# A gate-weight quarter read and split earlier, and three tiles' sums moved from VectorE to GpSimd

## The chip, the cores and the metric

The kernel runs on one core of a Trainium2 chip. Its engines each run their own instruction list in order: TensorE (PE) for matrix products, VectorE (DVE) and ScalarE (ACT) for elementwise work, GpSimd (POOL) for a few elementwise operations and the indexed transfers, SyncE (SP) as the queue that issues most reads and writes of HBM. They meet through semaphores. The metric is the device time of one execution in microseconds (us), lower is better.

## What is computed

One decoder layer over 512 tokens of width 1024: three parallel mixers with a shared projection, a mixture-of-experts layer, then a gated per-layer embedding and a final norm. The change lies where the expert layer hands over to the last stage, so of the reference only this part matters:

```python
h = h + mix @ w_out[i]
# top-1 group of 8 experts, top-2 experts in it: 32 experts, 256 wide
hid = silu(t @ w_gate[e]) * (t @ w_up[e]) * combine
h = h + sum over e of hid @ w_down[e]
gate = sigmoid(rmsnorm(h, ple_norm_g) @ ple_gate_w + ple_gate_b)      # 1024 x 1024
e = p @ ple_proj_w                                                    # 256 -> 1024
h = h + gate * e
return rmsnorm(h, final_norm_g)
```

## The kernel before

The 512 tokens are four tiles of 128 (`h1[0]` to `h1[3]`, 128 x 1024 float32, resident in SBUF). The 32 experts run as 16 pairs. For each pair the tokens that chose it are gathered into 64 slots an expert; `gate_up` (L997) forms the two hidden products, `down` (L1029) the output product. The weights of a pair are six reads of 1 MB each, issued in order by SP from `load_units` (L691); each waits for the one three before it.

The outputs of pairs 0 to 14 are written by an indexed transfer to `yd` in HBM, two rows a token. They come back as `ys[t]` (1 MB a tile, `load_y`, L1168), and `add_y` (L1164) adds both rows to `h1[t]`: two 128 x 1024 additions, both inputs in SBUF. Pair 15 does not go through HBM: its result stays on the chip as a high part and a low part (L1038 on ScalarE, L1039 on VectorE), and `scatter` (L1051) brings it to the tokens with products against a one-hot matrix, the result in PSUM, which L1053 adds to half of `h1[t]`.

The gate product (L1242) runs with each float32 operand split into a high part `h` and a low part `l`: three products hi·hi, hi·lo, lo·hi for each of the 8 slices `k` of 128 rows, 24 matmuls of 512 columns for half a tile. The weights come as four quarters of 1 MB (`gate_load`, L1060). `gate_hi(k, hf)` (L1071, ScalarE) writes the high part of one slice and half, `gate_lo(k, hf)` (L1075, VectorE) the low part: 16 of each. The tokens are transposed by `turn` (L1221), whose high part is written by ScalarE (L1223) and whose low part by VectorE (L1224).

`finish` then takes each tile in two halves (the last one in three pieces): L1252 scales the product out of PSUM and adds the bias row, L1253 is the sigmoid, L1254 multiplies by the embedding, L1255 adds `h1`, L1256 sums squares, L1257 multiplies by the final gain. On VectorE L1254, L1255 and L1257 have both inputs in SBUF; L1252, L1053, L1039 and L1224 have one of theirs in PSUM. `rms` prepares a tile's norm; the powers -1/2 (`rsp`, `rsl`, L63) run on GpSimd.

The embedding product (`ple`, L724) is made of 32 quarter steps, each two products of 128 x 256, one PSUM bank for four of them; `PLE` says how many stand in each pair, `PLE_LAST` how many behind the last one.

The order on SP and PE is the order of the code; from pair 14 on so is that of ScalarE and VectorE. GpSimd's order is chosen by the scheduler. `unit` takes a 1 MB slot of a ring of SBUF buffers, `free` gives it back. The tail: `tail` calls `last(t)` for each tile, which runs the gate products, and at given steps `(half, k)` calls `prep(t + 1)` (the next tile's transposes, splits and norm) and `sums(t + 2)`.

Of the kernel before, what the change touches and what calls it, by code (L numbers as in the profile page):

```python
# [14 lines left out]
ALU = mybir.AluOpType  # L15
# [6 lines left out]
KC = D // P  # L22
# [5 lines left out]

FILL = (8, 3, 0, 1, 0, 1, 0, 1, 0, 1, 1, 1, 4, 2, 2, 2, 9)

PLE = (5, 1, 1, 1, 1, 1, 1, 1, 1, 1, 1, 1, 1, 1, 2)
PLE_LAST = (4, 4, 4)
AHEAD = 3
NR, NL = 4, 9
CLEAR = (7, 8, 9, 10)
# [578 lines left out]
def ffn(ctx, tc, A, K, mixh, mixl, out, dbg, stage):  # L614

    nc = tc.nc
    V, SC, PE, G = nc.vector, nc.scalar, nc.tensor, nc.gpsimd
# [7 lines left out]
    h1 = K["h1"]  # L625
# [10 lines left out]
    def unit(dt, shape, slot=None):  # L636
        slot = slot or ring.pop(0)
        u = slot[0].tile(shape, dt, name="unit", tag=slot[1])
        slot_of[id(u)] = slot, u
        return u  # L640

    def free(*us):
        ring.extend(slot_of[id(u)][0] for u in us)

    def big(n, dt=F32, shape=(P, D)):
        return mw.tile(list(shape), dt, name="big", tag=f"big{n}")
# [20 lines left out]
    ps = K["ps"]  # L667
# [17 lines left out]
    def load_units(m=96):  # L685

        while ring and m and len(slab) < 96:
            n, m = len(slab), m - 1
            n = n - n % 6 + (0, 3, 1, 4, 2, 5)[n % 6]
            slab[n] = unit(F32, [P, 2048])  # L690
            loads.append(nc.sync.dma_start(slab[n], A["w_exp"][n // 3, n % 3]).ins)  # L691
            if len(loads) > AHEAD:
                tc.add_manual_dep(loads[-1], loads[-1 - AHEAD].name,
                                  mybir.DependencyInfo(mybir.DependencyClass.Sync, mybir.DependencyReason.DATA))
# [20 lines left out]
    def ple_steps():  # L715

        pT, pW = pl_in
        for j in range(8):
            t, hf = j // 2, j % 2
            p = ps("pe", "sc" if j < 5 else "gu")  # L720
            for c in range(2):
                for k in range(2):
                    n = hf * 512 + c * 256
                    PE.matmul(p[:, c * 256:c * 256 + 256], pT[:, k * S + t * P:k * S + (t + 1) * P], pW[:, k, n:n + 256],  # L724
                              start=(k == 0), stop=(k == 1))
                    if c == k == 1:
                        kept.append((t, hf, p))
                        ple_out()
                    yield

    def ple_out():

        while kept and kept[0][0] // 2 < len(eo):
            t, hf, p = kept.pop(0)
            SC.activation(eo[t // 2][:, t % 2, hf * 512:hf * 512 + 512], p, AF.Copy)  # L735
# [3 lines left out]
    def ple(n):  # L739
        for _ in range(n):  # L740
            next(ple_left, None)
# [131 lines left out]
    with tc.manual_schedule(engines={mybir.EngineType.PE}):  # L873
        for hf in range(2):
            part(hf, 0, WO_LATE[:2])
        for n in range(len(halves) - 1):
# [5 lines left out]
            if n >= 2:  # L882
                t, hf = halves[n - 2]
# [130 lines left out]
    def down(i, behind=lambda n: None):  # L1014
        w, hid = hid_[i]
        pT = ps("ht", "ht")[:, :256].rearrange("p (f n) -> p f n", f=2)
        hT = mw.tile([P, 2, P], F32, name="hidT", tag="hidT")
        for f in range(2):
            PE.transpose(pT[:, f], hid[:, f * P:(f + 1) * P], ident)
        SC.activation(hT, pT, AF.Copy)  # L1020
        behind(0)
        o = out_[i] = []
        if i < 15:
            o = big(1)
        for hf in range(2):
            dn = ps("dn", "dn")
            for f in range(2):
                for e in range(2):
                    PE.matmul(dn[64 * e:64 * e + 64], hT[:, f, 64 * e:64 * e + 64],  # L1029
                              w[e][2][:, 1024 * f + 512 * hf:1024 * f + 512 * hf + 512],  # L1030
                              start=(f == 0), stop=(f == 1))
            if i < 15:
                SC.activation(o[:, 512 * hf:512 * hf + 512], dn, AF.Copy)  # L1033
                continue
            if hf == 0:
                o2 = unit(F32R, [P, 4, 512])
            oh, ol = o2[:, 2 * hf], o2[:, 2 * hf + 1]
            SC.activation(oh, dn, AF.Copy)  # L1038
            V.tensor_tensor(ol, dn, oh.bitcast(F32), ALU.subtract)  # L1039
            o.append((oh, ol))  # L1040
            behind(1 + hf)
        if i < 15:
            G.indirect_dma_start(out=yd, out_offset=bass.IndirectOffsetOnAxis(ap=idy[:, i:i + 1], axis=0), in_=o, in_offset=None,  # L1043
                                 bounds_check=2 * S - 1, oob_is_err=False)

    def scatter(j):

        t, hf = j // 2, j % 2
        sc = ps("sc", "sc")
        for q in range(2):  # L1050
            PE.matmul(sc, DTs[15][:, t], out_[15][hf][q], start=(q == 0), stop=(q == 1))  # L1051
        y = h1[t][:, 512 * hf:512 * hf + 512]
        V.tensor_tensor(y, y, sc, ALU.add)  # L1053


    gr, gw = [], {}
# [1 line left out]
    def gate_load(j):  # L1058
        gr.append(unit(F32, [P, 4, 512]))
        nc.sync.dma_start(gr[j], A["ple_gate_w"][j])  # L1060

    def gate_part(k, hf):
        hs = slice(hf * 512, hf * 512 + 512)
        return gr[2 * hf + k // 4][:, k % 4], gw[k][:, 0, hs], gw[k][:, 1, hs]

    def gate_hi(k, hf):

        if hf == 0:
            gw[k] = unit(F32R, [P, 2, D])
        raw, h, _ = gate_part(k, hf)  # L1070
        SC.activation(h, raw, AF.Copy, scale=g3c[:, k:k + 1])  # L1071

    def gate_lo(k, hf):
        raw, h, l = gate_part(k, hf)
        V.scalar_tensor_tensor(l, raw, g3c[:, k:k + 1], h.bitcast(F32), ALU.mult, ALU.subtract)  # L1075
        if k % 4 == 3:
            free(gr[2 * hf + k // 4])
# [54 lines left out]
    def count_beyond():  # L1132
        on = ov["on"] = mw.tile([1, 1], I32, name="on")
        po = ps("pov", "xt")
        PE.matmul(po[:1, :1], ov["om"], ones[:, :1], start=True, stop=True)
        V.tensor_copy(on, po[:1, :1])
# [22 lines left out]
    ys = []  # L1159

    def add_y(t, rs=(0, 1)):

        for r in rs:
            V.tensor_tensor(h1[t], h1[t], ys[t][:, r], ALU.add)  # L1164

    def load_y(t):
        ys.append(unit(F32, [P, 2, D]))
        nc.sync.dma_start(ys[t], yd.rearrange("(r n) d -> n r d", r=2)[t * P:(t + 1) * P])  # L1168

    ends = ExitStack()  # L1170
    for i in range(16):
        if i == 14:
            ends.enter_context(tc.manual_schedule(engines={mybir.EngineType.Activation, mybir.EngineType.DVE}))
        gate_up(i, between(i))
        free(slab[6 * i + 1], slab[6 * i + 4])
        if i == 15:
            break
        if i in (3, 7):
            eo.append(unit(F32, [P, 2, D]))
            ple_out()  # L1180
        load_units()
        if i == 0:
            ple(PLE[0])
        gather_T(i + 1, 1)
        if i > 0:
            ple(PLE[i])
        down(i, lambda n: gather_T(i + 1, 0))
        free(slab[6 * i + 2], slab[6 * i + 5])
        load_units()
        if i == 14:  # L1190
            load_y(0)
            for j in range(4):
                gate_load(j)
            load_y(1)
            rows = mix.tile([P, 2, D], F32, name="rows", tag="m0")
            nc.sync.dma_start(rows[:, 0], bcast(A["ple_gate_b"]))
            load_y(2)
            nc.sync.dma_start(rows[:, 1], bcast(A["final_norm_g"]))
            load_y(3)
# [33 lines left out]
    def prep(t):  # L1233
        for hf in range(2):
            turn(t, hf)()
        rms(t)
# [37 lines left out]
    def tail(sums=None):  # L1274

        for t in range(NT):
            at = {}
            if t + 1 < NT:
                at[1, 1] = lambda: prep(t + 1)
            if sums and t == 0:  # L1280
                at[0, 6] = lambda: sums(1)
            if sums and t + 2 < NT:
                at[1, 5] = lambda: sums(t + 2)
            last(t, at)

    def sums(t):
        add_y(t)
        for hf in range(2):
            scatter(2 * t + hf)

    down(15, lambda n: n < 2 and add_y(0, (n,)))
    ple(PLE_LAST[0])
    gate_hi(0, 0)
    for hf in range(2):
        scatter(hf)
    gate_lo(0, 0)
    gate_hi(1, 0)
    ple(PLE_LAST[1])
    lo = [turn(0, hf) for hf in range(2)]
    ple(PLE_LAST[2])  # L1300
    free(pl_in[1])
    for f in lo:
        f()
    gate_lo(1, 0)
    for k in range(2, KC):
        gate_hi(k, 0)
        gate_lo(k, 0)
    count_beyond()
    for k in range(KC):
        gate_hi(k, 1)  # L1310
        gate_lo(k, 1)
    ov_slots = ring[:3]
    junk, h3s = (unit(F32, shape, slot) for shape, slot in zip(([P, 2, 512], [P, 4, 512]), ring[3:]))
    SC.preload_act_table_set("sigmoid_and_others")
    rms(0)
    tail(sums)
    ends.close()
# [157 lines left out]
```

## Time and profile before

| what | value |
|---|---|
| median of 3 runs | 557.77 us (557.16 to 558.68) |
| the profiled execution | 556.99 us, of which span 555.2 us |
| TensorE busy, mean | 514.5 us (93%) |
| VectorE busy | 276.2 us (50%) |
| ScalarE busy | 210.8 us (38%) |
| GpSimd busy | 87.1 us (16%) |
| read from HBM | 139.61 MB |

All times of rows are us from the start of the span. The stages: mixers up to about 250 us, the expert pairs to 477 us, the rest is the stage that the change touches. A row of the timeline is one instruction or a run of equal ones: its start, how long it or the run lasted, its engine and line, what it writes and reads, how many (x14), and in brackets how long the engine had sat idle before it and what it waited for. A mean over the span tells little here: VectorE is busy for half the span, but nearly all the time in the last 75 us.

### The profile page before, as it was taken

What the parts mean: (1) busy time and instruction counts of PE and PEld (TensorE: products, weight loads), DVE (VectorE), ACT (ScalarE), POOL (GpSimd) and SP (SyncE); (2) the same over time, 40 slices, a digit from 0 to 9 for tenths busy, and PEclk for the clock granted to TensorE, in tenths of its full rate; (3) what the DMA queues carried; (4) which work ended last, traced back from release to release, by engine and by line L of the source; (5) the groups of instructions that cost most, each with busy time, mean ns of one, the idle gap of its engine ahead of it and who ended that gap; (6) DMA issues with size and microseconds to landing.
All of it is one profiled execution on the core that took longest, in us unless ns stands there. A gap on an engine that the chain in (4) does not pass through costs nothing.

```text
span 555.2 us, 7581 instructions
## 1 busy us (share of the span) xinstructions
PE 514.5 (93%) x2713; PEld 325.3 (59%) x2713; DVE 276.2 (50%) x735; ACT 210.8 (38%) x443; POOL 87.1 (16%) x122
## 2 busy tenths in 40 slices
PE   8899999999999999999999999998798987949992
PEld 5797886876997788844333333332233332638872
DVE  6762957756747565773422322221121111597764
ACT  7466665646766434411112111110111101473352
POOL 3301111221008500002111111111110000011110
PEclk9999999999999999999999999999999999988997
DMA  8882222300339669989999999999999999950111
GB/s 303 265 325 73 62 72 71 91 26 2 117 126 418 251 263 413 348 337 387 416 412 417 399 394 387 375 383 396 368 399 418 416 418 390 416 211 0 40 44 73
DMA packets 35641, 148.82 MB, mean 268 GB/s; under 512 B 6557, under 2 KB 14109, under 8 KB 22160
## 3 DMA queue, kind: packets, MB, share of 16 engines
q1 hardware_dynamic: 29984, 137.46, 64.3%
q0 software_dynamic: 4320, 7.95, 3.8%
q10 hardware_dynamic: 1296, 2.89, 1.3%
q8 instruction: 23, 0.38, 0.3%
q14 instruction: 18, 0.15, 0.1%
HBM read 139.61 MB, written 16.25 MB: 281 GB/s over the span
## 4 chain that ended last, share of the span: by engine, by line
PE 62%; DMA 18%; DVE 9%; ACT 7%; issue 2%; POOL 1%; SPq 0%; ACTq 0%; DVEq 0%; POOLq 0%
DMA unit<-in_w_exp_dram 17%; PE gu L997 12%; PE pj L234 9%; PE po L80 8%; PE dn L1029 7%; PE pj L257 5%; PE z L257 4%; PE z L311 2%; PE po L333 2%; PE pe L724 2%; ACT unit L1071 2%; PE x L974 1%; DVE h L1164 1%; PE pl L780 1%; PE z L292 1%
## 5 line engine op out<-in xcount | busy, mean ns | idle before, releaser
L997 PE MATMUL gu<-unit,xT 128*64 128x512 f32 x512 | 127.5, 598 | 13.1 <-DMA unit<-in_w_exp_dram 13.1
L997 PEld LDWEIGHTS gu<-unit,xT 128*64 128x64 f32 x512 | 37.0, 137 | 85.0 <-issue 59.2
L1029 PE MATMUL dn<-unit,hidT 128*64 128x512 f32 x256 | 60.6, 599 | 1.7 <-ACT hidT L1020 0.8
L234 PE MATMUL pj<-xh,wp 128*128 128x512 f32 x176 | 51.2, 398 | 0.4 <-ACT wp L69 0.4
L1242 PE MATMUL pg<-unit 128*128 128x512 f32 (+1 forms) x216 | 47.9, 378 | 0.8 <-ACT unit L735 0.6
L1002 ACT ACTIVATE sg<-gu 128x256 f32<-128x256 f32 x16 | 6.1, 383 | 110.5 <-PE gu L997 110.5
L1003 DVE SCALAR_TENSOR_TENSOR hid<-sg,wsl,gu 128x256 f32<-128x256 f32 x16 | 7.7, 478 | 79.6 <-ACT sg L1002 79.5
L1242 PEld LDWEIGHTS pg<-unit 128*128 128x128 f32 x216 | 37.9, 193 | 9.0 <-ACT unit L735 0.7
L1043 POOL DMA_INDIRECT yd<-big,idy x15 | 15.1, 1009 | 163.8 <-ACT big L1033 163.8
L1029 PEld LDWEIGHTS dn<-unit,hidT 128*64 128x64 f32 x256 | 19.7, 137 | 32.0 <-issue 24.2
L234 PEld LDWEIGHTS pj<-xh,wp 128*128 128x128 f32 x176 | 32.6, 188 | 8.2 <-ACT wp L69 1.3
L1033 ACT ACTIVATE big<-dn 128x512 f32<-128x512 f32 x30 | 17.9, 597 | 50.0 <-PE dn L1029 50.0
L930 DVE COPY SL<-sl 128x10 f32<-128x10 f32 (+1 forms) x17 | 2.8, 167 | 66.0 <-PE sl L929 66.0
L70 DVE TENSOR_TENSOR wp<-wraw,wp 128x768 fp32r<-128x768 f32 (+2 forms) x28 | 25.8, 927 | 13.6 <-ACT wp L69 13.4
L69 ACT ACTIVATE wp<-wraw 128x768 fp32r<-128x768 f32 (+2 forms) x28 | 22.8, 817 | 20.2 <-PE pj L234 9.8
L234 PE MATMUL pj<-xl,wp 128*128 128x512 f32 x88 | 29.4, 401 | 0.0
L986 DVE TENSOR_TENSOR xT<-xt,g2c 128x512 f32<-128x512 f32 x30 | 20.6, 687 | 11.8 <-PE xt L985 11.7
L80 PE MATMUL po<-wo,mx 128*128 128x512 f32 x96 | 25.7, 408 | 0.0
L257 PE MATMUL pj<-wp,xh 128*128 128x384 f32 x96 | 24.8, 351 | 0.0
L80 PE MATMUL po<-unit,mx 128*128 128x512 f32 x96 | 24.1, 399 | 0.0
L943 POOL DMA_INDIRECT xg<-tnd,idx x15 | 15.4, 1029 | 33.7 <-issue 16.0
L985 PEld LDWEIGHTS xt<-ident,xg 128*128 128x128 f32 x120 | 13.4, 141 | 11.5 <-issue 11.4
(293 smaller groups left out, 881.2 us busy)
## 6 DMA issues: line engine op xcount, KB each, us to landing
unit<-in_w_exp_dram SPq DMA_DIRECT2D x96, 1024.0 KB, 8.7
wraw<-in_w_in_dram SPq DMA_DIRECT2D x20, 384.0 KB, 3.5
yd<-zero SPq DMA_DIRECT2D x4, 1024.0 KB, 7.9
unit<-yd SPq DMA_DIRECT2D x4, 1024.0 KB, 6.5
unit<-in_ple_gate_w_dram SPq DMA_DIRECT2D x4, 1024.0 KB
wraw<-in_w_out_dram SPq DMA_DIRECT2D x8, 256.0 KB, 3.0
h<-in_x_dram SPq DMA_DIRECT2D x4, 512.0 KB
unit<-in_w_out_dram SPq DMA_DIRECT2D x4, 512.0 KB, 7.8
```

What stands on the lines that cost most here:

```text
L69: nc.scalar.activation(h, src, AF.Copy)
L70: nc.vector.tensor_tensor(l, src, h.bitcast(F32), ALU.subtract)
L80: nc.tensor.matmul(p, a[k][:, ts_], K["wo"][k][:, b, hs], start=(n == 0), stop=(n == 3 * len(ks) - 1))
L234: PE.matmul(q, a[:, i * P:(i + 1) * P], b[k], start=(n == 0), stop=(n == 3 * KC - 1))
L257: PE.matmul(p[t][:, :W_IN[j]], a[k][:, t * P:(t + 1) * P], b, start=(n == 0), stop=(n == 3 * KC - 1))
L943: G.indirect_dma_start(out=xg[i % 2], out_offset=None, in_=tnd, in_offset=bass.IndirectOffsetOnAxis(ap=idx[:, i:i + 1], axis=0), bounds_ch ...
L986: V.tensor_tensor(xTs[i, hf], p.rearrange("p (a b) -> p a b", a=4), g2c[:, 4 * hf:4 * hf + 4, None].to_broadcast([P, 4, P]), ALU.mult)
L997: PE.matmul(gu[64 * e:64 * e + 64], xTs[i, k // 4][:, k % 4, 64 * e:64 * e + 64], w[e][k // 4][:, 512 * (k % 4):512 * (k % 4) + 512], star ...
L1029: PE.matmul(dn[64 * e:64 * e + 64], hT[:, f, 64 * e:64 * e + 64], w[e][2][:, 1024 * f + 512 * hf:1024 * f + 512 * hf + 512], start=(f == 0 ...
L1033: SC.activation(o[:, 512 * hf:512 * hf + 512], dn, AF.Copy)
L1043: G.indirect_dma_start(out=yd, out_offset=bass.IndirectOffsetOnAxis(ap=idy[:, i:i + 1], axis=0), in_=o, in_offset=None, bounds_check=2 * S ...
L1242: PE.matmul(p, hT[t][:, a, ks], gw[k][:, b, hs], start=start and n == 0, stop=stop and n == len(ab) - 1)
```

## The change

The first quarter of the gate weights is read before the rows of tile 0 instead of behind them. ScalarE loads the sigmoid table and splits that quarter's four slices between the copy of pair 15's transposed hidden state and the copies of its output; VectorE does three of the four low parts there. Eight of the twelve quarter steps of the embedding product that stood behind the last pair move into pairs 6 to 13. The sums of tiles 1, 2 and 3 (`add_y`, six instructions) go from VectorE to GpSimd; in the code they are called earlier. `scatter` now issues only its product and returns the addition, so tile 1's product stands ahead of the gate products and its two additions behind the last low part. In tile 0 `prep(1)` moves from step (1, 1) to step (1, 6), `sums(2)` keeps (1, 5), and `sums(1)` at (0, 6) is gone.

```diff
-PLE = (5, 1, 1, 1, 1, 1, 1, 1, 1, 1, 1, 1, 1, 1, 2)
-PLE_LAST = (4, 4, 4)
+PLE = (5, 1, 1, 1, 1, 1, 2, 2, 2, 2, 2, 2, 2, 2, 2)
+PLE_LAST = 4
...
-            p = ps("pe", "sc" if j < 5 else "gu")
+            p = ps("pe", "sc" if j < 7 else "gu")
...
-        V.tensor_tensor(y, y, sc, ALU.add)
+        return lambda: V.tensor_tensor(y, y, sc, ALU.add)
...
-            V.tensor_tensor(h1[t], h1[t], ys[t][:, r], ALU.add)
+            (G if t else V).tensor_tensor(h1[t], h1[t], ys[t][:, r], ALU.add)
...
         if i == 14:
+            gate_load(0)
             load_y(0)
-            for j in range(4):
-                gate_load(j)
+            gate_load(1)
             load_y(1)
+            gate_load(2)
+            gate_load(3)
...
             if t + 1 < NT:
-                at[1, 1] = lambda: prep(t + 1)
-            if sums and t == 0:
-                at[0, 6] = lambda: sums(1)
+                at[1, 1 if t else 6] = lambda: prep(t + 1)
             if sums and t + 2 < NT:
+                at[0, 0] = lambda: add_y(t + 2)
                 at[1, 5] = lambda: sums(t + 2)
...
-    down(15, lambda n: n < 2 and add_y(0, (n,)))
-    ple(PLE_LAST[0])
-    gate_hi(0, 0)
...
+    def behind_down(n):
+        if n == 0:
+            SC.preload_act_table_set("sigmoid_and_others")
+            for k in range(4):
+                gate_hi(k, 0)
+            for k in range(3):
+                gate_lo(k, 0)
+        if n < 2:
+            add_y(0, (n,))
+
+    down(15, behind_down)
+    ple(PLE_LAST)
+    for f in [scatter(hf) for hf in range(2)]:
+        f()
+    gate_lo(3, 0)
     lo = [turn(0, hf) for hf in range(2)]
...
+    add_y(1)
     for f in lo:
         f()
-    gate_lo(1, 0)
-    for k in range(2, KC):
+    second = [scatter(2 + hf) for hf in range(2)]
+    for k in range(4, KC):
         gate_hi(k, 0)
         gate_lo(k, 0)
-    count_beyond()
     for k in range(KC):
         gate_hi(k, 1)
         gate_lo(k, 1)
+    for f in second:
+        f()
+    count_beyond()
...
-    SC.preload_act_table_set("sigmoid_and_others")
     rms(0)
     tail(sums)
```

In the rows of the order `unit` is a ring slot, `dn`, `pe`, `sc`, `xt` and `pg` are PSUM banks, `h_1_1509` is `h1[1]`, `ms` and `rsp` are columns of the norm. ScalarE behind the last pair, from the copy of its transposed hidden state (`hidT`) to the table load, the difference of the two orders:

```order
 L1020 ACTIVATE hidT<-ht 128x256
+L1293 ACT_TABLE_LOAD
+L1071 ACTIVATE unit<-unit,g3c 128x512 x4
 L1038 ACTIVATE unit<-dn 128x512 x2
 L735 ACTIVATE unit<-pe 128x512
-L1071 ACTIVATE unit<-unit,g3c 128x512 x2
-L735 ACTIVATE unit<-pe 128x512
-L1223 ACTIVATE unit<-xt 128x512 x2
-L735 ACTIVATE unit<-pe 128x512
-L1071 ACTIVATE unit<-unit,g3c 128x512 x14
-L1314 ACT_TABLE_LOAD
```

The table load and four of the sixteen high parts now stand ahead of the copies of the last output (L1038), and two of the copies of the embedding product (L735) are gone from here.

VectorE from the low parts of tile 0's transpose to the first step of `finish`, before:

```order
L1224 TENSOR_TENSOR unit<-xt,unit 128x512 x2
L1075 SCALAR_TENSOR_TENSOR unit<-unit,g3c 128x512 x7
L1136 CAST on<-pov 1x1
L1075 SCALAR_TENSOR_TENSOR unit<-unit,g3c 128x512 x8
L1208 TENSOR_SCALAR ms<-pm 128x1
L1210 SCALAR_TENSOR_TENSOR ms<-pm,ms 128x1
L1164 TENSOR_TENSOR h_1_1509<-h_1_1509,unit 128x1024 x2
L1053 TENSOR_TENSOR h_1_1509<-h_1_1509,sc 128x512 x2
L1252 SCALAR_TENSOR_TENSOR unit<-pg,rsp,rows 128x512
```

and now:

```order
L1226 TENSOR_TENSOR unit<-xt,unit 128x512 x2
L1075 SCALAR_TENSOR_TENSOR unit<-unit,g3c 128x512 x12
L1053 TENSOR_TENSOR h_1_1509<-h_1_1509,sc 128x512 x2
L1136 CAST on<-pov 1x1
L1210 TENSOR_SCALAR ms<-pm 128x1
L1212 SCALAR_TENSOR_TENSOR ms<-pm,ms 128x1
L1254 SCALAR_TENSOR_TENSOR unit<-pg,rsp,rows 128x512
```

Twelve low parts are left instead of fifteen, the two sums of tile 1 (L1164) are gone, and the two additions from PSUM stand ahead of the norm. (From here on the changed kernel's lines are two higher: L1252 is now L1254.)

GpSimd behind its last indexed transfer, the difference:

```order
 L943 DMA xg<-tnd,idx 128x1024
 L1043 DMA yd<-big,idy 1024x1024 x2
+L1164 TENSOR_TENSOR h_1_1509<-h_1_1509,unit 128x1024 x2
+L1164 TENSOR_TENSOR h_2_1510<-h_2_1510,unit 128x1024
+L63 TENSOR_TENSOR rsp<-ms,mhalf 128x1
+L1164 TENSOR_TENSOR h_2_1510<-h_2_1510,unit 128x1024
+L1164 TENSOR_TENSOR h_3_1511<-h_3_1511,unit 128x1024 x2
+L63 TENSOR_TENSOR rsp<-ms,mhalf 128x1
+L63 TENSOR_TENSOR rsl<-ms,mhalf 128x1
```

Three of the six sums stand ahead of tile 0's power (`rsp`), three behind it; nothing but the arrival of their rows and their own order holds them back.

## Rows read from the trace of the kernel before

**Rows 1.** Queue SP: timeline from 400 us (start, us, what), then its waits (total, times, longest).

```profile
401.44 62.83 SPq L691 DMA_DIRECT2D unit<-in_w_exp_dram  x24
...
SPq L691 <- DMA unit<-in_w_exp_dram: 39.9, 17, 3.2
```

**Rows 2.** Timeline, 472 to 485 us: start, us, instruction, count, idle time before it.

```profile
472.72 0.38 ACT L1020 ACTIVATE hidT<-ht 128x256 f32<-128x256 f32 x1 [1.05 <-PE ht L1019]
...
474.75 1.23 DVE L1164 TENSOR_TENSOR h<-h,unit 128x1024 f32<-128x1024 f32 x1 [2.57 <-DMA unit<-yd]
...
475.14 0.60 ACT L1038 ACTIVATE unit<-dn 128x512 fp32r<-128x512 f32 x1 [2.04 <-PE dn L1029]
...
479.25 1.29 DVE L1053 TENSOR_TENSOR h<-h,sc 128x512 f32<-128x512 f32 x2 [0.94 <-PE sc L1051]
...
482.10 1.89 PE L724 MATMUL pe<-unit,big 128*128 128x256 f32 x8
...
482.55 1.29 DVE L1224 TENSOR_TENSOR unit<-xt,unit 128x512 fp32r<-128x512 f32 x2 [1.35 <-ACT unit L1223]
```

**Rows 3.** Timeline, 484 to 500 us.

```profile
484.52 8.68 ACT L1071 ACTIVATE unit<-unit,g3c 128x512 fp32r<-128x512 f32 x14
...
489.32 5.37 DVE L1075 SCALAR_TENSOR_TENSOR unit<-unit,g3c 128x512 fp32r<-128x512 f32 x8
...
493.23 1.28 ACT L1314 ACT_TABLE_LOAD   x1
...
495.96 2.48 DVE L1164 TENSOR_TENSOR h<-h,unit 128x1024 f32<-128x1024 f32 x2
496.13 1.48 POOL L63 TENSOR_TENSOR rsp<-ms,mhalf 128x1 f32<-128x1 f32 x1 [34.43 <-DVE ms L1210]
498.54 1.29 DVE L1053 TENSOR_TENSOR h<-h,sc 128x512 f32<-128x512 f32 x2
```

**Rows 4.** Timeline of the tail: first step of each half tile, and others.

```profile
499.75 0.74 DVE L1252 SCALAR_TENSOR_TENSOR unit<-pg,rsp,rows 128x512 f32<-128x512 f32 x1
...
501.25 0.69 DVE L1254 TENSOR_TENSOR unit<-unit 128x512 f32<-128x512 f32 x1 [0.76 <-ACT unit L1253]
...
514.56 0.74 DVE L1252 SCALAR_TENSOR_TENSOR unit<-pg,rsp,rows 128x512 f32<-128x512 f32 x1
...
529.25 0.74 DVE L1252 SCALAR_TENSOR_TENSOR unit<-pg,rsp,rows 128x512 f32<-128x512 f32 x1
...
540.16 0.74 DVE L1252 SCALAR_TENSOR_TENSOR unit<-pg,rsp,rows 128x512 f32<-128x512 f32 x1
...
546.38 0.48 DVE L1252 SCALAR_TENSOR_TENSOR unit<-pg,rsp,rows 128x256 f32<-128x256 f32 x1
...
549.04 0.54 POOL L63 TENSOR_TENSOR rsl<-ms,mhalf 128x1 f32<-128x1 f32 x1 [9.38 <-DVE ms L1210]
```

**Rows 5.** Timeline of earlier stages: GpSimd and VectorE elementwise work side by side.

```profile
10.01 0.75 DVE L179 SCALAR_TENSOR_TENSOR xl<-xr,g,xh 128x512 fp32r<-128x512 f32 x1 [0.18 <-ACT xh L178]
...
16.13 2.04 POOL L183 TENSOR_TENSOR gs<-gs,xr 128x512 f32<-128x512 f32 x1 [2.07 <-ACT xr L181]
...
16.94 1.78 DVE L179 SCALAR_TENSOR_TENSOR xl<-xr,g,xh 128x512 fp32r<-128x512 f32 x1
...
175.14 2.38 POOL L677 TENSOR_TENSOR unit<-unit 128x1024 fp32r<-128x1024 f32 x1
175.26 0.69 DVE L85 TENSOR_TENSOR h<-h,po 128x512 f32<-128x512 f32 x1 [0.17 <-PE po L80]
```

**Rows 6.** Matmuls of the tail (timeline), then stretches: busy by engine, granted clock, DMA.

```profile
499.29 1.97 PE L1221 MATMUL xt<-ident,h 128*128 128x128 f32 x8 [7.18 <-DVE h L1053]
...
505.91 8.50 PE L1242 MATMUL pg<-unit 128*128 128x512 f32 x36
...
492.00:497.00 5.00, 0.11 (x1) 0.00 (x0) 3.96 (x8) 3.83 (x7) 0.87 (x1) 0.97 0.26 104
497.00:500.00 3.00, 0.71 (x4) 0.71 (x5) 2.86 (x5) 0.00 (x0) 0.61 (x1) 0.50 0.00 0
```

More of the change, by code (lines that the diff above doesn't have):

```diff
@@ L1286, in sums @@
     def sums(t):
-        add_y(t)
         for hf in range(2):
-            scatter(2 * t + hf)
-    down(15, lambda n: n < 2 and add_y(0, (n,)))
-    ple(PLE_LAST[0])
-    gate_hi(0, 0)
[L1294 to L1298, printed above, removed]
+            scatter(2 * t + hf)()
+    def behind_down(n):
[12 more added lines that the diff above has]
+    gate_lo(3, 0)
     lo = [turn(0, hf) for hf in range(2)]
-    ple(PLE_LAST[2])
     free(pl_in[1])
+    add_y(1)
     for f in lo:
         f()
-    gate_lo(1, 0)
-    for k in range(2, KC):
+    second = [scatter(2 + hf) for hf in range(2)]
+    for k in range(4, KC):
         gate_hi(k, 0)
         gate_lo(k, 0)
-    count_beyond()
     for k in range(KC):
```

## The prediction

> **What bounds the kernel now.** I read the read queue first. From 401.44 us it issues 24 reads of 1 MB in 62.83 us, 2.62 us each, and in the last part it waits for nothing but earlier reads [rows 1]. So up to pair 15 the stream of weights is the bound, and TensorE work there is free as long as it fits between reads. Then the timeline behind the last pair [rows 2]: ScalarE copies the hidden state until 473.10, tile 0's rows land at 474.75, the output is split, added to tile 0 by 479.25 + 1.29 = 480.54, and the transpose's low parts are done at 482.55 + 1.29 = 483.84. Then [rows 3]: ScalarE writes the last 14 high parts in 8.68 us (0.62 each), VectorE the last eight low parts in 5.37 us (0.67 each), ending at 489.32 + 5.37 = 494.69, behind ScalarE's 493.20. VectorE is the later of the two. Table load, norm, the sums of tile 1 (2.48) and its additions from PSUM (1.29) follow, and tile 0 is finished from 499.75 on. The tail is VectorE's step by step [rows 4]: the tiles start at 499.75, 514.56, 529.25 and 540.16, so 14.81, 14.69 and 10.91 us apart, and the last piece at 546.38, 6.22 later. The third distance is shorter by about what tile 3 no longer has: 2.48 + 1.29 = 3.77. So every microsecond off VectorE counts here until TensorE is the later one. TensorE needs 8.50/36 = 0.236 us a matmul [rows 6], 48 x 0.236 = 11.3 us a tile, plus about 1 us of transposes (eight took 1.97 at a halved clock) and about 1 us for the four products of a later tile: 13.4 us, only 1.3 below VectorE's 14.7.
>
> **The sum's frame.** It is made on the profiled execution: its time is 556.99, span 555.2, 1.8 around it. What follows the last piece (546.38 to 555.2) is not changed. The median of the runs, 557.77, is 0.78 above that execution, so I add the change of the last piece's start to 557.77.
>
> **Quarter steps of the embedding product.** Eight steps of 1.89/4 = 0.47 us [rows 2] leave the stage behind the last pair, one each for pairs 6 to 13. There the queue waits for reads only [rows 1], so they cost 0; without that cover, 8 x 0.47 = 3.8. What they give is in the ladder below, since ScalarE and VectorE set that stage.
>
> **The quarter read ahead.** It stands behind all weights in one queue, so I charge the weights nothing; if reads shared the bandwidth, up to one read's 2.62. It takes the place of tile 0's rows: it lands at or a little ahead of 474.75, since it doesn't wait for pair 14's output to be written. Tile 0's rows land one read later, 477.3 at most, tile 1's two reads after that, at about 482, tile 2's near 491.5 (two more quarters, half a read of bias rows and their own 1 MB), tile 3's near 495.
>
> **Behind the last pair.** ScalarE: 473.10, table load 1.28 [rows 3], four high parts 2.5, so the two output copies start at 476.9 instead of 475.14 and end at 478.1. VectorE: three low parts from 475.1 to 477.2, where it had mostly waited; two sums of 1.23 and two splits of 0.68, 481.0; two additions, 482.3 instead of 480.54. That is 1.8 late. The fourth low part and the transpose's two end at 484.2 instead of 483.84. Twelve low parts at 0.67 then end at 492.2, against 494.69: **2.5 saved**, if nothing holds VectorE.
>
> **The sums on GpSimd.** This is the term that decides. GpSimd takes 2.38 us for an operation of this shape with two inputs [rows 5], VectorE 2.48/2 = 1.24 [rows 3]; six of them are 14.3 us. The question is what VectorE does meanwhile. In an early stage, GpSimd ran an addition until 16.13 + 2.04 = 18.17; VectorE's split of the very form of the low part (both inputs in SBUF) had started at 16.94 and took 1.78 us instead of 0.75: it ended 0.55 behind GpSimd [rows 5]. An addition with one input in PSUM ran in 0.69 us right through a GpSimd operation of 2.38 [rows 5]. And GpSimd's tiny power took 1.48 us while VectorE added two SBUF rows [rows 3], 0.54 when it didn't [rows 4]. So the two exclude each other when VectorE reads two inputs from SBUF, and the one that waits gets its turn at the next end of an instruction. The Trainium skill says the same ("SBUF — State Buffer", Who interferes with whom): VectorE with two SBUF inputs contends with a GpSimd instruction that reads SBUF, and the second fully blocks until the first ends; by that rule the sums come out as forecast here, and the trace agrees (1.78 against 0.75). Its "Perfetto Trace Analysis" (Optimizing Scalar/DVE Operations) warns that moving work between these two engines might not help.
>
> Each sum therefore costs VectorE between 0 (beside a step on PSUM, or a wait) and about 2.2 us (2.38 less the start-up that overlaps), against 1.24 before. Placed by the arrivals: tile 1's first sum asks near 482, beside additions and low parts from PSUM: I take 0.8. Its second one, and tile 2's first near 491.5, fall into low parts: 2.2 each. Together 5.2, so the low parts end at 492.2 + 5.2 = 497.4. Two additions from PSUM 1.2, norm columns 0.4, power 0.54 and its hand-over: tile 0 starts at 499.6 instead of 499.75, **0.15 saved**. The 2.5 gained by the early quarter and the 2.48 of tile 1's sums go into the holding.
>
> **Tile 0.** Its 14.81 us lose 2.48 of sums and 0.6 of waits (the additions now stand where VectorE waited for ScalarE). The three sums left on GpSimd start with the tile. In L1254, L1255, L1257 VectorE reads two SBUF inputs, and each must wait for a sum: the first ends 0.55 behind 2.3, the second at 5.65, the third at 8.4 us instead of 3.65: 4.75 added. 14.81 - 2.48 - 0.6 + 4.75 = 16.5.
>
> **Tiles 1 to 3.** VectorE would need 14.69 - 2.48 = 12.2, but TensorE begins a tile only when its transposed low parts are there and needs 13.4, of which it is ahead by some tenths: 13.0. Tile 2 has no additions: 11.3 + 1 = 12.3 of TensorE instead of 10.91, since it is no longer ahead. The last step stays 6.2. **Sum:** 499.6 + 16.5 + 13.0 + 12.3 + 6.2 = 547.6 against 546.38, 1.2 later: 557.77 + 1.2 = **559.0**.
>
> **The rivals.**
> *No holding* (chance 0.15): GpSimd's long additions leave VectorE alone. For it: the short spans of GpSimd are rough in a profile. Against: the rows above. Low parts end at 492.2, tile 0 starts at 494.5, its step is 11.6 (VectorE without sums and waits), then 13.0, 12.3, 6.2: 537.6, 8.8 earlier, 549.0.
> *Half of it* (0.12): VectorE wins its turns, and sums fall beside steps on PSUM or waits for the sigmoid (0.76 in each half [rows 4]). If half of the 5.2 and 4.75 goes, 5.0 us: 554.0.
> *The clock of TensorE* (0.28), the slower side. Between tile 0's last product, near 501, and tile 1's low parts, near 509.5, TensorE has almost nothing. In the trace of before it had one matmul in 492 to 497; the granted clock was then 0.50 in 497 to 500 [rows 6], which is 1.2 GHz instead of 2.4, and eight transposes took 1.97. If tile 1's first 4 us of products run at that level they lose 2 us; 0.4 is slack, 1.6 counts, since tiles 1 and 2 are TensorE's: 560.6. It decides where such a gap arises again; the one before, 7.18 us of waiting, came ahead of the transposes [rows 6].
> *The quarter comes late* (0.05): if it lands a read later, at 477.3, the output copies and all behind shift by up to 2; part of it hides in the holding: 560.
>
> **How the numbers follow.** The forecast has 0.40. A measurement can tell about 0.3% from no change, 1.67 us, so the bounds are 556.1 and 559.4; the forecast lies just inside. Its uncertainty is about 1.5 us, mostly where tile 1's rows land: 1 us later or earlier moves the end by as much. Slower: 0.35 of the forecast, 0.8 of the clock, 0.6 of the late quarter, 0.39. Faster: the first rival, 0.8 of the second, a little of the forecast, 0.27. The rest, 0.34, is within. The range leaves out no holding below and the worst of the clock case above: 552.5 to 562.0.
>
> **What would show it.** Low parts (L1075) of 2.9 us instead of 0.74, two or three of them, and three steps of 1.4 us and more in tile 0's first half, each ending 0.55 behind a GpSimd sum; tile 0 starting near 499.6; tiles 16.5, 13.0 and 12.3 apart, TensorE without idle time in tiles 1 and 2. Right on the clock rival: a granted clock of 0.5 near 510. Wrong: low parts at 0.74 throughout and a start near 494.5.

## The result and the profile of the changed kernel

The changed kernel took 559.73 us (median of 6 runs, 558.47 to 562.25), the kernel before 556.94 in the same comparison: ratio 1.0055, 95% interval 1.0029 to 1.0081. It is slower by a little, by about 3 us. A second comparison (run e12 below) gave 1.0054 [1.0027, 1.0082].

The end of the weight stream moves by a microsecond or two from execution to execution, and all behind it moves along. So positions are counted here from the copy of pair 15's transposed hidden state, 472.72 in the kernel before [rows 2] and 471.65 in the changed one. From there to the last piece the kernel before takes 546.38 - 472.72 = 73.66, the changed one 547.91 - 471.65 = 76.26: 2.6 later. A position is read from one traced execution, a ratio from the medians of several.

The changed kernel's timeline behind the last pair; the columns are as in [rows 2], L1075 are the low parts, L1164 the sums:

```profile
471.65 0.38 ACT L1020 ACTIVATE hidT<-ht 128x256 f32<-128x256 f32 x1 [1.04 <-PE ht L1019]
...
474.24 2.56 ACT L1071 ACTIVATE unit<-unit,g3c 128x512 fp32r<-128x512 f32 x4 [0.91 <-DMA unit<-in_ple_gate_w_dram]
...
481.73 2.96 DVE L1075 SCALAR_TENSOR_TENSOR unit<-unit,g3c 128x512 fp32r<-128x512 f32 x1
...
485.82 11.10 DVE L1075 SCALAR_TENSOR_TENSOR unit<-unit,g3c 128x512 fp32r<-128x512 f32 x12
```

and GpSimd beside it:

```profile
481.78 5.16 POOL L1164 TENSOR_TENSOR h<-h,unit 128x1024 f32<-128x1024 f32 x2 [19.25 <-DMA unit<-yd]
490.53 2.52 POOL L1164 TENSOR_TENSOR h<-h,unit 128x1024 f32<-128x1024 f32 x1 [3.60 <-DMA unit<-yd]
```

The low part that starts beside GpSimd's first sum takes 2.96 us; in a run of them they stood 0.67 apart [rows 3], and a single one without a sum beside it takes 0.74. The next twelve take 11.10 where a version without sums (e2) takes 8.05. Together (2.96 - 0.74) + (11.10 - 8.05) = 5.3 us of holding. By sums it is 2.2 for the first, 0.9 for the second, which holds only the first of the twelve (it ends at 481.78 + 5.16 = 486.94), and 2.1 for the third, which starts at 490.53.

VectorE and GpSimd at tile 0, then the first step of the later tiles and of the last piece (L1254 is L1252 of the kernel before, and so on):

```profile
499.13 7.89 POOL L1164 TENSOR_TENSOR h<-h,unit 128x1024 f32<-128x1024 f32 x3
499.18 0.75 DVE L1254 SCALAR_TENSOR_TENSOR unit<-pg,rsp,rows 128x512 f32<-128x512 f32 x1 [0.68 <-POOL rsp L63]
...
500.69 1.37 DVE L1256 TENSOR_TENSOR unit<-unit 128x512 f32<-128x512 f32 x1 [0.76 <-ACT unit L1255]
502.10 2.71 DVE L1257 TENSOR_TENSOR unit<-unit,h 128x512 f32<-128x512 f32 x1
504.84 2.73 DVE L1259 TENSOR_TENSOR unit<-unit,rows 128x512 f32<-128x512 f32 x1
...
516.77 0.75 DVE L1254 SCALAR_TENSOR_TENSOR unit<-pg,rsp,rows 128x512 f32<-128x512 f32 x1 [1.41 <-PE pg L1244]
...
529.70 0.75 DVE L1254 SCALAR_TENSOR_TENSOR unit<-pg,rsp,rows 128x512 f32<-128x512 f32 x1 [0.47 <-PE pg L1244]
...
541.69 0.75 DVE L1254 SCALAR_TENSOR_TENSOR unit<-pg,rsp,rows 128x512 f32<-128x512 f32 x1 [0.45 <-PE pg L1244]
...
547.91 0.48 DVE L1254 SCALAR_TENSOR_TENSOR unit<-pg,rsp,rows 128x256 f32<-128x256 f32 x1
```

The three steps with two SBUF inputs take 1.37, 2.71 and 2.73 instead of 0.69 each [rows 4]: 4.74 more. The tiles are 17.59, 12.93 and 11.99 apart and the last piece 6.22 behind, against 14.81, 14.69, 10.91 and 6.22 [rows 4]. In [rows 4] no step waits for TensorE; here the first step of tiles 1, 2 and 3 does.

TensorE's timeline where tile 1 begins, and three stretches (columns: stretch, its length, busy of PE, PEld, DVE, ACT, POOL, granted clock, DMA share, GB/s):

```profile
500.23 1.64 PE L1244 MATMUL pg<-unit 128*128 128x512 f32 x6
...
506.16 0.73 PE L1244 MATMUL pg<-unit 128*128 128x512 f32 x2 [4.29 <-ACT unit L1225]
509.48 7.93 PE L1244 MATMUL pg<-unit 128*128 128x512 f32 x25 [2.60 <-DVE unit L1226]
```

```profile
504.00:508.00 4.00, 0.73 (x2) 0.30 (x2) 3.96 (x4) 2.91 (x8) 2.94 (x2) 0.85 0.00 0
508.00:512.00 4.00, 2.52 (x6) 2.04 (x7) 3.19 (x8) 0.63 (x1) 0.55 (x1) 0.50 0.00 0
512.00:516.00 4.00, 4.00 (x15) 3.17 (x15) 2.51 (x5) 1.34 (x3) 0.55 (x1) 0.80 0.00 0
```

TensorE stands still for most of 501.9 to 509.5. It first waits for tile 1's high parts, which ScalarE writes (L1225) only behind the squares of a step that VectorE ended late, then for tile 1's low parts, which VectorE itself reaches late (L1226). When it returns it runs at a granted clock of 0.50, the 1.2 GHz level, and the 25 products take 7.93 us, against 6.08 in a kernel where the clock stays at 1.00 (e2): 1.85 lost.

### The profile page after: what moved, and what is told of

It is laid out like the page before. It is cut to its first block, busy times and chain, and to the rows that moved or that the text cites. A ratio compares the mean times of both kernels' runs of the same rounds, so it can differ in the third digit from the quotient of the medians.

```text
span 556.7 us, 7586 instructions
## 1 busy us (share of the span) xinstructions
PE 515.1 (93%) x2713; PEld 325.4 (58%) x2713; DVE 280.0 (50%) x729; ACT 210.5 (38%) x443; POOL 99.9 (18%) x128
## 4 chain that ended last, share of the span: by engine, by line
PE 60%; DMA 25%; DVE 7%; issue 3%; ACT 3%; POOL 1%; SPq 0%; ACTq 0%; DVEq 0%; POOLq 0%
DMA unit<-in_w_exp_dram 18%; PE gu L997 10%; PE pj L234 9%; PE po L80 7%; PE dn L1029 6%; PE pg L1244 5%; PE pj L257 5%; PE z L257 4%; PE z L311 2%; DMA unit<-in_ple_gate_w_dram 2%; PE po L333 2%; DMA tnd<-big 2%; DVE unit L1075 1%; DMA yd<-big,idy 1%; DMA xr<-in_xT_dram 1%
## 5 line engine op out<-in xcount | busy, mean ns | idle before, releaser
L1244 PE MATMUL pg<-unit 128*128 128x512 f32 (+1 forms) x216 | 49.9, 390 | 6.9 <-ACT unit L1225 4.3
L1244 PEld LDWEIGHTS pg<-unit 128*128 128x128 f32 x216 | 39.5, 200 | 18.2 <-ACT unit L1225 4.7
L1029 PEld LDWEIGHTS dn<-unit,hidT 128*64 128x64 f32 x256 | 18.1, 136 | 33.7 <-issue 25.4
```

The costliest lines, as they stand in the source:

```text
L1244: PE.matmul(p, hT[t][:, a, ks], gw[k][:, b, hs], start=start and n == 0, stop=stop and n == len(ab) - 1)
```

## The experiments

Theory: GpSimd's sums hold every VectorE step that has two inputs in SBUF, and the late tile 1 then costs TensorE its clock. Rivals: the early quarter or the new order is at fault; the sums cost the same wherever they run; any GpSimd work slows VectorE; the clock is hidden. Each run was compared with the kernel before on the same chip. In the table, positions are from the copy of the hidden state (ACT L1020) of the same execution; "restart" is TensorE's first product that needs tile 1's low parts from VectorE.

| kernel | ratio, 95% interval | tile 0 starts | restart behind it | 25 products | last piece |
|---|---|---|---|---|---|
| before | 1 | 27.03 | | | 73.66 |
| changed | 1.0055 [1.0029, 1.0081] | 27.53 | 10.30 | 7.93 | 76.26 |
| changed again (e12) | 1.0054 [1.0027, 1.0082] | 27.54 | 10.31 | 7.83 | 76.18 |
| sums on VectorE (e1) | 0.9948 [0.9925, 0.9970] | 26.83 | 5.77 | 6.08 | 70.01 |
| the same again (e8) | 0.9915 [0.9887, 0.9943] | 25.78 | 5.77 | 7.01 | 69.05 |
| no sums (e2) | 0.9877 [0.9850, 0.9904] | 22.10 | 5.78 | 6.08 | 64.46 |
| quarter only (e3) | 0.9960 [0.9937, 0.9984] | 24.74 | | | 71.39 |
| sums only (e4) | 1.0078 [1.0051, 1.0105] | 31.89 | | | 76.64 |
| pause filled, 30 (e5) | 1.0025 [0.9999, 1.0050] | 27.48 | | | 75.48 |
| pause filled, 24 (e11) | 1.0009 [0.9987, 1.0032] | 27.51 | | | 74.47 |
| write only (e6) | 0.9850 [0.9799, 0.9901] | 22.48 | 5.78 | 7.62 | 66.39 |
| beside PSUM (e7) | 0.9938 [0.9917, 0.9958] | 26.05 | 5.77 | 7.38 | 69.69 |
| sums later (e9) | 0.9931 [0.9907, 0.9955] | 24.69 | 5.78 | 7.62 | 69.90 |
| later and filled (e10) | 0.9924 [0.9903, 0.9946] | 24.42 | | | 71.18 |

e1 and e8 are one kernel, and yet tile 0 starts 1.05 apart in them. Two arrivals make up most of it: ScalarE's first high part starts 2.59 behind the copy in e1 and 2.10 in e8, and in e1 VectorE waits another 0.47 for tile 0's rows. (That first high part starts 2.22 behind in e2, 2.57 to 2.61 behind in all others that read the quarter early.) So a difference of about 1 in the last column is read below only where the steps of the two traces show where it arises.

### Where the sums run (e1, e8, e2)

```diff
-            (G if t else V).tensor_tensor(h1[t], h1[t], ys[t][:, r], ALU.add)
+            V.tensor_tensor(h1[t], h1[t], ys[t][:, r], ALU.add)
```

> The changed kernel with the six sums of tiles 1 to 3 back on VectorE, at the places in the order where the change calls them; all else as changed. Holding theory (a GpSimd sum keeps VectorE from steps with two SBUF inputs): no low part over 0.8 us, low parts end near 494.7 instead of 496.9, tile 0 starts near 497 and takes about 14.3; some 4 to 5 us below the changed kernel, 2 below before. Rival, TensorE's gap and clock are the cost: the sums take 7.4 us of VectorE again and the gap stays, so no better than the changed kernel. Rival, the order of the reads is the cost: the same as the changed kernel.

> The changed kernel with all sums on VectorE once more, on the same chip as the version with two sums beside PSUM steps, to compare those two: 0.993 to 0.997 of the kernel before, all low parts at 0.74.

In e2 `add_y` returns at once for tiles 1 to 3, so their returned rows are never added:

> The changed kernel without the sums of tiles 1 to 3 on any engine: the rows come back but are not added, so the output lacks experts 0 to 29 for those tiles. Holding theory: low parts all near 0.74 us and ending near 492, tile 0 from 494.5, about 9 us below the changed kernel, 549 to 551. Rival, clock or reads: the sums on GpSimd cost nothing by themselves, so within 2 us of the changed kernel.

VectorE and TensorE in e1 (two sums, twelve low parts, the 25 products):

```profile
484.86 2.48 DVE L1164 TENSOR_TENSOR h<-h,unit 128x1024 f32<-128x1024 f32 x2
...
488.45 8.03 DVE L1075 SCALAR_TENSOR_TENSOR unit<-unit,g3c 128x512 fp32r<-128x512 f32 x12
```

```profile
506.15 6.08 PE L1244 MATMUL pg<-unit 128*128 128x512 f32 x25 [0.76 <-DVE unit L1226]
```

and in e2, the low parts and the 25 products:

```profile
486.08 8.05 DVE L1075 SCALAR_TENSOR_TENSOR unit<-unit,g3c 128x512 fp32r<-128x512 f32 x12
```

```profile
502.17 6.08 PE L1245 MATMUL pg<-unit 128*128 128x512 f32 x25 [0.76 <-DVE unit L1227]
```

One line turns a kernel 0.55% slower than before into one 0.5 to 0.85% faster, with every low part back at 0.74 to 0.75. Against e2 the six sums cost 70.01 - 64.46 = 5.6 us (4.6 by e8) on VectorE and 76.26 - 64.46 = 11.8 on GpSimd. The 11.8 splits in the table: tile 0 starts 5.43 later, the restart is 4.53 later behind it, the 25 products take 1.85 longer; 11.81 in all. Of the 5.43, 0.37 is the quarter, which came that much earlier in e2; the rows account for the rest as holding and clock. In e1 the quarter came as late as in the changed kernel, and the last piece is still 76.26 - 70.01 = 6.25 earlier. e1 also keeps the new order of the calls, so that order is not at fault.

### The two halves of the change (e3, e4)

e3 keeps the early quarter, the moved embedding steps, the table load and the splits, with sums, additions and tail as before. e4 is the kernel before with only the sums moved:

```diff
-            V.tensor_tensor(h1[t], h1[t], ys[t][:, r], ALU.add)
+            (G if t else V).tensor_tensor(h1[t], h1[t], ys[t][:, r], ALU.add)
```

> Only the first half of the change: quarter read ahead, its splits behind the last pair, the table load there, the quarter steps of the embedding product moved; sums on VectorE and tail as before. Holding theory: 2.5 us below before (the three low parts moved, the table load gone from the path): 554 to 555. Rival, the reads' order costs: tile 0's rows come a read later and the output copies wait, so the same as before or slower, 557 to 559.

> Only the second half: the kernel before with the sums of tiles 1 to 3 on GpSimd, nothing else moved. Holding theory: three to four sums fall into low parts (2.2 us each), two into tile 0's first half, against 7.4 us taken from VectorE: tile 0 starts 3 to 5 us later than before, in all 3 to 6 us slower than before, 560 to 563. Rival without holding: VectorE loses 7.4 us of work, 551 to 553.

GpSimd and VectorE in e4:

```profile
485.48 11.04 POOL L1164 TENSOR_TENSOR h<-h,unit 128x1024 f32<-128x1024 f32 x4 [24.71 <-DMA unit<-yd]
```

```profile
491.54 9.51 DVE L1075 SCALAR_TENSOR_TENSOR unit<-unit,g3c 128x512 fp32r<-128x512 f32 x8
...
504.95 2.77 DVE L1255 TENSOR_TENSOR unit<-unit,h 128x512 f32<-128x512 f32 x1
```

The early quarter alone gains: tile 0 starts 27.03 - 24.74 = 2.29 earlier and the tail behind it is unchanged (14.82, 14.70, 10.91, 6.22). The sums alone lose: all four early ones fall among low parts, eight of which take 9.51 instead of 5.37 [rows 3]; the six ahead of these take 8.34 instead of 4.07, so the four sums hold VectorE for 8.4, 2.1 each. So the change is a gain of 2.3 and a loss that is larger.

### What of a sum holds VectorE (e6, e7)

e6 replaces each of the six sums by a write of as many zeros, which reads nothing; the returned rows of tiles 1 to 3 are not added:

```diff
-            (G if t else V).tensor_tensor(h1[t], h1[t], ys[t][:, r], ALU.add)
+            if t:
+                G.memset(ys[t], 0.0)
+            else:
+                V.tensor_tensor(h1[t], h1[t], ys[t][:, r], ALU.add)
```

> The changed kernel with each of GpSimd's six sums replaced by a write of zeros to as many elements of the returned rows' tile (two rows of 1024 at once, so it reads nothing); the returned rows of tiles 1 to 3 aren't added. Theory (GpSimd and VectorE hold each other where VectorE reads two SBUF inputs and GpSimd reads two as well): all low parts at 0.74, tile 0's additions at 0.69, the tail as in the kernel without sums, ratio 0.988 to 0.990. Rival (any GpSimd instruction that goes through SBUF holds VectorE for its own length): low parts and additions of up to 1.8 us more each, ratio 0.995 to 1.005.

GpSimd, VectorE and TensorE in e6:

```profile
481.68 3.69 POOL L1165 MEMSET unit<- 128x2048 f32 x2 [19.43 <-DMA unit<-yd]
...
493.94 5.41 POOL L1165 MEMSET unit<- 128x2048 f32 x3
```

```profile
483.70 8.04 DVE L1075 SCALAR_TENSOR_TENSOR unit<-unit,g3c 128x512 fp32r<-128x512 f32 x12
...
496.25 0.69 DVE L1260 TENSOR_TENSOR unit<-unit,h 128x512 f32<-128x512 f32 x1
...
506.77 0.75 DVE L1257 SCALAR_TENSOR_TENSOR unit<-pg,rsp,rows 128x512 f32<-128x512 f32 x1 [1.11 <-PE pg L1247]
```

```profile
499.79 7.62 PE L1247 MATMUL pg<-unit 128*128 128x512 f32 x25 [0.77 <-DVE unit L1229]
```

GpSimd writes for 3.69 us across the start of the low parts and for 5.41 us through tile 0, and VectorE's steps stay at 0.67 apart and 0.69. It is GpSimd's reading that holds VectorE, not its presence. (A sum reads two inputs; a GpSimd instruction that reads only one was not run. The last piece is 1.93 later than in e2: 0.38 at tile 0's start, since the quarter came 0.39 later, and 7.62 - 6.08 = 1.54 of clock.) The Trainium skill ("SBUF — State Buffer", Who interferes with whom) says so too: a step with two SBUF inputs contends with a GpSimd instruction that reads SBUF, not with one that only writes it. These rows agree with it.

e7 takes e1 and moves two of the six sums to GpSimd, where VectorE reads PSUM: tile 1's first row beside the transpose's splits from PSUM, tile 3's first row tied behind the first half of tile 0's mean square. `add_y` now also takes the rows and the engine, VectorE where none is named.

```diff
-    gate_lo(3, 0)
     lo = [turn(0, hf) for hf in range(2)]
...
-    add_y(1)
+    add_y(1, (0,), G)
     for f in lo:
         f()
+    gate_lo(3, 0)
+    add_y(1, (1,))
...
-                at[0, 0] = lambda: add_y(t + 2)
+                at[0, 0] = lambda: add_y(t + 2, (0, 1) if t == 0 else (1,))
```

> The sums put where VectorE reads PSUM: tile 1's first row on GpSimd ahead of the low parts of the last gate rows, which now stand behind the transposes' low parts; tile 3's first row on GpSimd behind the first half of tile 0's mean square, beside VectorE's additions from PSUM; the other four sums on VectorE, as in the version with all sums on VectorE. Theory (a GpSimd sum beside steps with a PSUM input costs nothing): two VectorE sums of about 1.2 us less in the path, last low parts 0.74, 2.4 us below the version with all sums on VectorE: ratio 0.990 to 0.991. Rival (it costs as much wherever it runs): the same as all sums on VectorE, 0.995, or slower; a two-SBUF step of VectorE then shows 2 us or more.

In e7 GpSimd's first sum and the low part that meets its end, then its second sum and VectorE beside it and later:

```profile
481.22 2.38 POOL L1164 TENSOR_TENSOR h<-h,unit 128x1024 f32<-128x1024 f32 x1 [19.38 <-DMA unit<-yd]
...
483.25 0.90 DVE L1075 SCALAR_TENSOR_TENSOR unit<-unit,g3c 128x512 fp32r<-128x512 f32 x1
```

```profile
501.14 2.39 POOL L1164 TENSOR_TENSOR h<-h,unit 128x1024 f32<-128x1024 f32 x1 [4.75 <-DVE ms L1220]
```

```profile
500.98 1.27 DVE L1053 TENSOR_TENSOR h<-h,sc 128x512 f32<-128x512 f32 x2
502.17 1.28 DVE L1236 TENSOR_TENSOR unit<-xt,unit 128x512 fp32r<-128x512 f32 x2
...
522.58 0.75 DVE L1264 SCALAR_TENSOR_TENSOR unit<-pg,rsp,rows 128x512 f32<-128x512 f32 x1 [0.47 <-PE pg L1254]
```

The mechanism held: the sums take 2.38 and 2.39, their undisturbed length, and VectorE's steps on PSUM beside the second take 1.27 and 1.28 for two, as in e1. Only a low part that began before the first sum had ended took 0.90 instead of 0.74; it ended 0.55 behind the sum. The gain did not come: 2.4 was expected, and the ratio is that of e1 and e8. Tile 0's step is 1.25 shorter than in e1 (12.70 against 13.95), but the next two are 12.74 and 11.98 against 12.10 and 10.91, and VectorE now waits for TensorE in them. In e1 and e8 it never does. TensorE also came back at a lower clock than in e1, 7.38 for the 25 products instead of 6.08, and by the rule that follows 1.3 of the missing gain is that. Besides, a sum taken off VectorE behind the restart was no longer on the path.

This gives the tail one rule. In the five rows of the table where VectorE waits for TensorE in the last tiles and TensorE runs through (changed, e12, e2, e6, e7), the last piece stands 30.5 behind the end of the 25 products: 27.53 + 10.30 + 7.93 + 30.5 = 76.26, and likewise 76.18, 64.46, 66.38, 69.70. From the restart TensorE sets the end unless VectorE is later, as in e1. In e8 TensorE lost 0.9 to the clock (7.01) and VectorE's tail is that of e1 all the same (13.95, 12.11, 10.99, 6.22): where VectorE is the later one, the clock is hidden.

### The clock (e5, e11, e12)

e5 and e11 put 30 and 24 extra products into TensorE's pause; what they write is overwritten.

```diff
         def products(j, p, hs):
+            if t == 1 and j == 0:
+                for _ in range(24):
+                    PE.matmul(p, hT[0][:, 0, :P], gw[0][:, 0, :512], start=True, stop=True)
```

> The changed kernel with 30 extra products in TensorE's queue ahead of the first products of tile 1's tail; they use tile 0's hT and the gate's first rows, and what they write is overwritten by the first product that counts. They fill TensorE's pause, which lasted from 501.9 to about 509 us in the trace of the changed kernel, and behind which the granted clock was 0.50. Theory of the clock (1.1 of tile 0's 17.59 us were TensorE coming back at half rate): clock 1.00 in the stretch behind the pause, tile 0's step about 16.5 instead of 17.59, no wait of 1.4 us for pg at tile 1's start, time about 1.1 us below the changed kernel's: ratio to the kernel before 1.0035. Rival (the clock is hidden, VectorE sets the step alone): the clock rises, tile 0's step stays at 17.6, ratio 1.0055.

> The changed kernel with 24 instead of 30 extra products ahead of tile 1's first products, since 30 ran on past the point at which the restart was due (509.2 where 10.3 us behind tile 0's first piece gave 508.4). Theory of the clock: 25 products behind the restart in 6.1 us instead of 7.93, tile 0's step 15.8 to 16.5, last piece 1.4 to 1.9 us earlier than in the changed kernel, ratio 1.001 to 1.003. Rival (the clock costs 0.8 or less): as with 30 products, ratio 1.0025 or more.

> The changed kernel unchanged, on the same chip as its version with 24 extra products: ratio 1.003 to 1.008, tile 0's step 17.3 to 17.8 with the granted clock at 0.5 in part of the stretch behind the restart.

TensorE in e5, then in e11 (L1271 are the extra products; the 27 behind them are the two that need only tile 1's high parts and the 25):

```profile
502.16 7.16 PE L1271 MATMUL pg<-unit 128*128 128x512 f32 x30
509.16 6.40 PE L1244 MATMUL pg<-unit 128*128 128x512 f32 x27
```

```profile
505.57 5.77 PE L1271 MATMUL pg<-unit 128*128 128x512 f32 x24
511.17 6.75 PE L1244 MATMUL pg<-unit 128*128 128x512 f32 x27
```

With 24, tile 0's step falls from 17.49 to 16.20 and the last piece from 76.18 to 74.47, 1.7 earlier; on the same chip the ratio goes from 1.0054 to 1.0009. The granted clock in 508 to 516 is 1.00 here and in e5, and 0.54 and 0.60 in its two halves in e12. So the clock was not hidden in the changed kernel, and more than half of the 2.6 that the change lost was its price. With 30 the clock came back just as well, but the extra products ended at 509.2, behind the point at which the restart was due (498.06 + 10.30 = 508.36), and of the 1.7 only about 0.8 was left.

### Using it (e9, e10)

e9 is e7 with tile 2's sums moved from ahead of tile 0's first piece to ahead of tile 1's, behind the restart, and tile 3's second row to ahead of tile 2's; e10 adds 12 extra products.

```diff
-            if sums and t + 2 < NT:
-                at[0, 0] = lambda: add_y(t + 2, (0, 1) if t == 0 else (1,))
+            if sums and 1 <= t < NT - 1:
+                at[0, 0] = lambda: add_y(t + 1, (0, 1) if t == 1 else (1,))
+            if sums and t + 2 < NT:
```

> The version with two sums beside PSUM steps, with tile 2's two sums moved from ahead of tile 0's first piece to ahead of tile 1's, and tile 3's second row from there to ahead of tile 2's. Theory from the traces so far (TensorE runs without a pause from its second restart of tile 1 to the end, so the last piece starts 36.6 us after that restart plus what half rate costs; VectorE work ahead of the restart counts in full, behind it not until VectorE is the later one): tile 0's first piece at 24.4 to 24.8 us from the last hidT instead of 26.05, the restart 5.8 behind it, the last piece at 67.5 to 68.3 instead of 69.7; ratio 0.989 to 0.992 where that version had 0.9938. Rival (VectorE's sum of work sets the end, whatever the order): the sums moved cost as much later, last piece at 69.7, ratio 0.994.

> The same, with 12 extra products in TensorE's pause ahead of tile 1's first products that wait for the split; what they write is overwritten by the first product that counts. Theory of the clock: no half rate behind the restart (25 products in 6.1 us instead of 7.0 to 7.6), last piece 0.9 to 1.5 us earlier than without them, ratio 0.986 to 0.990. Rival (the clock is no part of the end): as without them.

VectorE's sums and TensorE's transposes of tile 2 in e9:

```profile
507.78 2.48 DVE L1164 TENSOR_TENSOR h<-h,unit 128x1024 f32<-128x1024 f32 x2
```

```profile
510.41 1.07 PE L1233 MATMUL xt<-ident,h 128*128 128x128 f32 x8 [0.79 <-DVE h L1164]
```

and in e10:

```profile
511.76 1.94 PE L1233 MATMUL xt<-ident,h 128*128 128x128 f32 x8 [2.34 <-DVE h L1164]
513.35 3.79 PE L1254 MATMUL pg<-unit 128*128 128x512 f32 x12
```

Tile 0 and the restart came as early as expected (24.69, 5.78 behind), the last piece did not: 69.90 where 67.5 to 68.3 was expected. The ratio, 0.9931, does not decide between theory and rival. By the rule above the last piece would stand at 24.69 + 5.78 + 7.62 + 30.5 = 68.6, so half rate makes up part of the miss. The other 1.3 is mostly waiting: tile 2's transposes need the sums that were moved, and TensorE, ahead of them, waited 0.79, and 0.16 again at tile 3's. In the traced execution of e10 the filled pause kept the clock, TensorE came to those transposes even earlier, waited 2.34, and lost the clock there: the granted clock in 512 to 516 was 0.63, the eight transposes took 1.94 and the next twelve products 3.79, where e7 took 1.04 and 3.03. There the saving went into a new pause. That execution took 554.85 us where the median of e10 is 552.75, and by the medians e9 and e10 cannot be told apart, so how much of it holds for the others is not shown. All versions that add every row and leave no GpSimd sum beside a run of VectorE steps with two SBUF inputs (e1, e3, e7 to e10) lie between 0.9915 and 0.9960, and their intervals overlap; the simplest, the changed kernel with its sums on VectorE, beats both kernels and nothing tried beats it measurably.

## Why the prediction was right, and where not

**The holding** was right in its mechanism. For tile 0, 4.75 us were forecast and 4.74 came, in the three steps named. For the low parts, 5.2 were forecast and 5.3 came, but there the total agrees partly by luck: 0.8, 2.2 and 2.2 were written for the three sums, and 2.2, 0.9 and 2.1 came. The first sum met a low part at its very start, where the forecast had steps on PSUM; the second ran beside the transpose's low parts from PSUM and held VectorE only at its end. VectorE's step ended 0.55 behind each sum, as forecast from [rows 5]: the sums at tile 0 end at 501.51 and 504.26, the steps at 500.69 + 1.37 = 502.06 and 502.10 + 2.71 = 504.81. "No holding" and "half of it" fell.

**The quarter read ahead** was forecast at or ahead of 474.75, 2.0 behind the copy of the hidden state. ScalarE was to start on it 1.66 behind, and started 474.24 - 471.65 = 2.59 behind, after a wait of 0.91. The low parts then ended 496.92 - 471.65 = 25.27 behind instead of 24.68, and tile 0 started at 27.53 instead of 26.88. That term was 0.6 short: a mild form of the rival "the quarter comes late", but the read did not come a whole read later.

**The tail** was forecast at 16.5 + 13.0 + 12.3 + 6.2 = 48.0 and took 17.59 + 12.93 + 11.99 + 6.22 = 48.73, and this near agreement hides two errors. The forecast left out TensorE's clock as the less likely case; it came, with 0.50 granted near 510 as that rival's sign said, and cost 1.7 to 1.85, where 1.6 was written. And without it the tail is 1.0 shorter than the forecast had it: 16.20 + 12.55 + 11.99 + 6.22 = 46.96 in e11. Each of the first three steps was put 0.3 to 0.45 too high, and the clock hid it.

**The sum.** In the trace the last piece came 2.6 later than before; the forecast was 1.2, the clock rival 2.8. As a ratio the forecast was 559.0/557.77 = 1.0022, which lies below the measured interval; the rival, 560.6/557.77 = 1.0051, lies in it. The median of 559.73 is near the forecast because the kernel before also ran 0.8 faster in this comparison. That nearness is luck. Counted from the copy, the last piece was forecast at 547.6 - 472.72 = 74.88 and came at 76.26: 0.65 from tile 0's start and 1.8 from the clock, less the 1.0 by which the rest of the tail was put too high. So the rival that had 0.28 is what happened, on top of the forecast's holding, and giving it less than the forecast was the wrong step: [rows 6] had shown the same loss behind a pause of 7.18, and the forecast itself left TensorE idle from 501 to 509.5. The sign, slower, had the largest chance, and the claim that the gain of the early quarter goes into the holding is shown by e3 and e4.

## What to carry to other kernels

Before moving elementwise work from VectorE to GpSimd, look at what VectorE does at that very time: beside steps that read PSUM a sum on GpSimd was free, beside steps with two SBUF inputs it cost 0.7 to 2.2 us, 10.0 for the six, where VectorE would have done each in 1.2. Delay on one engine is priced twice if it opens a pause in TensorE: here a restart that came 4.5 us late through holding cost 1.8 more through the clock. And a microsecond counts only on the engine that is later from there on; after the restart of tile 1 that changed from VectorE to TensorE as soon as one sum was gone.

## What the runs showed of the hardware

A write of 128 x 2048 zeros took GpSimd 1.8 us and did not slow VectorE at all (e6), while a sum of 128 x 1024 held a step that began within its first 0.7 us for 2.0 to 2.2, and one that began in its second half for 0.7 to 0.9 (changed kernel).

The holding goes both ways: among VectorE's steps a sum took GpSimd up to 2.79 instead of 2.37 (499.13: three in 7.89), and its power over 128 numbers 1.48 beside VectorE's sums [rows 3] but 0.57 in the changed kernel without them.

The length of the pause alone does not say whether the clock falls. TensorE's products that need only tile 1's high parts, in e2 and in e6:

```profile
500.67 0.73 PE L1245 MATMUL pg<-unit 128*128 128x512 f32 x2 [1.23 <-ACT unit L1226]
```

```profile
498.30 0.73 PE L1247 MATMUL pg<-unit 128*128 128x512 f32 x2 [1.19 <-ACT unit L1228]
```

In e2 TensorE paused 1.23 there and 0.76 ahead of the 25 products, and these took 6.08; in e6 it paused 1.19 and 0.77, and they took 7.62, with a granted clock of 0.57 in 500 to 504 where e2 had 1.00. What tells these two apart was not found and stays open; so the loss behind pauses this short could only be given as between 0 and 1.5 us. Behind the changed kernel's 4.29 and 2.60 it was 1.85.
